# Merging two scan directions in lockstep: five groups of small products per pair, with tiles per direction

## The chip, the cores and the metric

The kernel runs on one core of one Trainium2 chip, as one launch. The metric is the time of one execution on the device in microseconds, as the median of several runs. The engines are TensorE (PE in the profile, with its weight loads as PEld), VectorE (DVE), ScalarE (ACT), GpSimd (POOL) and SyncE (SP), whose queue issues most of the transfers.

## The reference

One layer of a backbone, for 512 latent tokens and 128 context tokens (640 columns in all) of width 2048. The part that matters here:

```python
def _delta_scan(r, w, k, v, aa, bb, s0, reverse):
    def step(S, inp):
        r_t, w_t, k_t, v_t, a_t, b_t = inp
        sa = jnp.einsum('bhvk,bhk->bhv', S, a_t)
        S = S * w_t[:, :, None, :] + sa[..., None] * b_t[:, :, None, :] + v_t[..., None] * k_t[:, :, None, :]
        return S, jnp.einsum('bhvk,bhk->bhv', S, r_t)
    s_fin, ys = lax.scan(step, s0, xs, reverse=reverse)

def _rwkv7_bidir(p, s0, lp):        # 16 heads of 64, scanned forward (d = 0) and backward (d = 1)
    for d in range(2):
        ...
        y, s_fin = _delta_scan(rh, decay, kd, vh, -kk, kk * heads(a), s0[:, d], reverse=(d == 1))

def _layer(x, mod, s0, shift_fn, lp):
    h = _rmsnorm(x, lp['norm1_g']) * (1.0 + sc1) + sh1
    p = h @ lp['w_in']
    o_a, s_fin = _rwkv7_bidir(shift_fn(p[..., :C_SHIFT], lp['mu_shift']), s0, lp)
    o_b = _chunk_gmlp(jax.nn.gelu(p[..., C_SHIFT:]), lp)
    x = x + g1 * (jnp.concatenate([o_a, o_b], axis=-1) @ lp['w_out'])
    ...
    ff = (jax.nn.silu(h @ lp['w_ffn_gate']) * (h @ lp['w_ffn_up'])) @ lp['w_ffn_down']
```

## The kernel before

The program has three long parts. First the input norm and the product with `w_in`; then the scans with the product with `w_out`; then the two feed-forward products. Matrix products in full precision are made of three products of split operands (a high part and a rest), so that each step of the first part is three **wide products** of 128x320 (lines 189, 190 and 191, tile `big`). The change lies in the first part, in what the profile has from about 320 to 1110 us.

The scan is computed in chunks of 64 tokens. For each chunk and head a 64x64 triangular matrix has to be inverted. Heads are handled two at a time: a *pair* `p` is two heads on 128 partitions, and there are eight pairs, each with two directions `d` and ten chunks. For each pair three generators make the work:

- `take_k` forms the operands of the pair and the triangular matrices: products `pG` (line 650), transposes `pXT` (668), products `pW` (682). At the end of it the 16x16 diagonal blocks go out to DRAM (`dd`, line 690, on POOL's queue).
- `solve` reads them back in another layout (`mix`, line 795) and inverts the 16x16 blocks on VectorE, row by row (lines 803 and 805, tiles `mx`), for both directions at once. The result goes out as `d2` (812).
- `merge` reads `d2` into `TB` (822) and puts the blocks together, from 16 to 32 and from 32 to 64, with small products of 32x32: five groups per direction, called groups 1 to 5 here. Group 1 is `blk(A1, Tn)`, group 2 `blk(TT, M1, (0, 2))`, group 3 `blk(M1, TT)`, all at line 840 (tile `pblk`); group 4 is line 865 (`pM`), group 5 line 874 (`pT`). Each group is emptied from PSUM by ScalarE (lines 847, 868, 877) or VectorE (853, 857) before the next can use it. The result `TF` goes to the record `d_S` (879, POOL's queue), which the second part reads.

What sets the order: three `Mixer` objects hold the generators and hand out their steps between wide products. `mixM` holds `merge`. A step's yielded number is its cost, which is paid from a budget that grows at every second wide step; `yield -1.0` puts the next step off to a place that no other step shares (the last wide step of a half of a window, so that groups are at least 12 wide products apart in the code), and `yield HOLD` waits for 68 wide steps. `take_k` may run `mixM` on by itself where `GB` buffers would run out (`mixM.until`). Behind this a list scheduler orders the instructions of each engine by its own estimates, so that the order on an engine is not quite that of the code. PSUM tiles of tag `pt` have two buffers; the groups share them with the transposes `pvt`, `pw`, `ptm` and the products `psp`. `M1` and `M2` share one buffer of tag `M1`, and `TF` has one.

Of the kernel before, what the change touches and what calls it, by code (L numbers as in the profile page):

```python
# [10 lines left out]
F32 = mybir.dt.float32  # L11
F32R = mybir.dt.float32r
BF16 = mybir.dt.bfloat16
AF = mybir.ActivationFunctionType
# [5 lines left out]
P = 128  # L20
# [5 lines left out]
CH = 64  # L26
NCH = T // CH
# [17 lines left out]
SDIV = 9.0  # L45
HOLD = 68
WAIT = 20
SUBST = 4.6
MODR = 1.36
NREC = 8  # L50
# [34 lines left out]
F_R, F_G, F_X, F_Z, F_T, REC = 0, 128, 256, 384, 512, 576  # L85
# [3 lines left out]
def flow_step(ctx: ExitStack, tc, x_prompt, x_sample, state_rwkv, c, c_ctx, w_mod, b_mod,  # L89
# [4 lines left out]
    V, S, G, TE = nc.vector, nc.scalar, nc.gpsimd, nc.tensor  # L94
# [22 lines left out]
    for h in range(2):  # L117
        s = slice(CH * h, CH * h + CH)
# [34 lines left out]
    d_S = dp.tile([NPAIR, P, 2, NCH, REC], F32, name="d_S")  # L153
# [51 lines left out]
    with ExitStack() as ph:  # L205
# [92 lines left out]
        for t in range(NT):  # L298
# [7 lines left out]
            for q in range(4):  # L306
                pt = ps0.tile([P, 4, P], F32, tag="pt", name="ptx")
# [470 lines left out]
    mlo = bk.tile([P, 1], F32, name="mlo", bufs=1)  # L778
# [3 lines left out]
    A1_ = bp.tile([P, 2, NCH, 32], F32, name="A1_")  # L782
    TB = bp.tile([P, 2, NCH, 2, 32], F32, name="TB")
# [33 lines left out]
    def merge(p, d2):  # L817

        GB = pairs[p].GB
        for gq in range(8):  # L820
            b = 16 * (gq % 2)
            BQ.dma_start(TB[16 * gq:16 * gq + 16, :, :, :, b:b + 16].rearrange("p d c w b -> p (d c w) b"),
                         d2[gq].rearrange("d c w a b -> a (d c w) b"))
        for h in range(2):
            base = 64 * (1 - h)
            for d in range(2):
                S.copy(A1_[base:base + 16, d, :, 16:32], GB[d][base:base + 16, :, 16:32])
                S.copy(A1_[base + 32:base + 48, d, :, 16:32], GB[d][base + 32:base + 48, :, 48:64])
        yield HOLD
        for d in range(2):  # L830
            GBd = GB[d]
            TF = bp.tile([P, NCH, CH], F32, tag="TF", name="TF")
            Tn, TT, A1 = TB[:, d, :, 0, :], TB[:, d, :, 1, :], A1_[:, d]

            def blk(lhs, rhs, rows=range(4)):
                ps = pt_.tile([P, NCH, 32], F32, tag="pt", name="pblk")
                for cc in range(NCH):
                    for a_ in rows:
                        s = slice(32 * a_, 32 * a_ + 32)
                        TE.matmul(ps[s, cc, :], lhs[s, cc, :], rhs[s, cc, :], start=True, stop=True,  # L840
                                  tile_position=(32 * a_, 32 * a_))
# [5 lines left out]
            S.copy(M1, ps)  # L847
            yield 1.6
            yield -1.0

            ps = blk(TT, M1, (0, 2))
            for h in range(2):
                V.tensor_add(Tn[lo32(h)], ps[lo32(h)], Tn[lo32(h)])
            yield 1.6
            yield -1.0
            ps = blk(M1, TT)
            V.tensor_add(TF[:, :, 32:64], ps, TT)
            S.activation(TF[:, :, 0:32], TF[:, :, 32:64], AF.Copy, scale=mlo[:, 0:1])
            yield 1.7
            M2 = bp.tile([P, NCH, 32], F32, tag="M1", name="M2")  # L860
            yield -1.0
            ps = pt_.tile([P, NCH, 32], F32, tag="pt", name="pM2")
            for cc in range(NCH):
                for h in range(2):
                    TE.matmul(ps[hi32(h), cc, :], GBd[lo32(h), cc, 32:64], Tn[lo32(h), cc, :],
                              start=True, stop=True, tile_position=(64 * (1 - h), 64 * (1 - h) + 32))
            for h in range(2):
                S.copy(M2[hi32(h), :, :], ps[hi32(h), :, :])
            yield 1.2
            yield -1.0  # L870
            ps = pt_.tile([P, NCH, 32], F32, tag="pt", name="pT2")
            for cc in range(NCH):
                for h in range(2):
                    TE.matmul(ps[lo32(h), cc, :], M2[hi32(h), cc, :], TF[hi32(h), cc, 32:64],
                              start=True, stop=True, tile_position=(64 * (1 - h) + 32, 64 * (1 - h)))
            for h in range(2):
                S.copy(TF[lo32(h), :, 32:64], ps[lo32(h), :, :])
            yield 1.2
# [91 lines left out]
    pt_ = pbx.enter_context(tc.tile_pool(name="pt_", bufs=2, space=PSUM))  # L970
# [452 lines left out]
    with ExitStack() as ph:  # L1423
# [695 lines left out]
```

## Time and profile before

| | us |
|---|---|
| median of 3 runs | 3245.55 (3244.21 to 3252.82) |
| the profiled execution | 3255.98 |
| its span in the profile | 3254.2 |

The profiled execution is 10.43 us longer than the median. "Busy" is the time in which an engine had an instruction running; matmul ends are modelled. A row of the timeline gives the start in the span, the length, the engine, the line and the operation, with the idle time of the engine ahead of it and what ended that in brackets. A matmul of plain 32-bit floats is recorded twice, so that a group of 20 small products has x40 and one of 40 has x80; wide products are recorded once. PEclk is the granted TensorE clock as a share of full speed.

### The profile page before, as it was taken

Reading aid. Unit: us, or ns where it says so; the run is one execution under the profiler, and the core shown is the slowest. Engines: PE = TensorE matmul, PEld = TensorE weight load, DVE = VectorE, ACT = ScalarE, POOL = GpSimd, SP = SyncE. Lnnn points to the kernel's source line nnn. Section 1 sums busy time; section 2 is a strip of 40 time slices with the busy share of each in tenths; the row PEclk is TensorE's granted clock in tenths of the full one; section 3 lists DMA queues with packets and bytes.
Section 4 is the critical chain, followed back from the end, with each engine's and each line's share of the span. In section 5 each row is a group of like instructions: output and inputs, shape, how many; then the busy total and the mean of one; then the engine's idle time right before and its main releaser. Section 6 shows DMA issues by size and latency. Waiting matters only on the chain.

```text
span 3254.2 us, 72319 instructions
## 1 busy us (share of the span) xinstructions
PE 3113.8 (96%) x28216; PEld 2872.8 (88%) x28216; DVE 2365.7 (73%) x4115; ACT 1459.9 (45%) x3197; POOL 1218.3 (37%) x1065
## 2 busy tenths in 40 slices
PE   6999999999999999999999999999999999999997
PEld 3687778777777888899899999999999999999997
DVE  4548766676676677766878778777777787887788
ACT  3344444454344444345644444444444445443365
POOL 2001121211112113422356655665665645454542
PEclk9999999999999999999999999999999999999999
DMA  9666676777678588654444344344344364553453
GB/s 371 222 197 197 192 217 181 197 205 193 184 194 227 159 275 269 200 173 151 129 130 122 106 129 127 103 128 127 108 124 121 117 189 150 162 155 105 150 165 120
DMA packets 740438, 550.88 MB, mean 169 GB/s; under 512 B 141056, under 2 KB 673504, under 8 KB 731264
## 3 DMA queue, kind: packets, MB, share of 16 engines
q1 hardware_dynamic: 727136, 532.47, 54.2%
q0 software_dynamic: 10624, 13.23, 1.8%
q8 instruction: 222, 3.64, 0.5%
q14 instruction: 120, 0.98, 0.1%
q10 hardware_dynamic: 2336, 0.57, 0.1%
HBM read 437.79 MB, written 110.95 MB: 169 GB/s over the span
## 4 chain that ended last, share of the span: by engine, by line
PE 72%; DVE 10%; DMA 7%; issue 6%; POOL 3%; ACT 2%; SPq 0%; DVEq 0%; POOLq 0%; ACTq 0%
PE P L1637 15%; PE P L1635 15%; PE P L1636 15%; PE big L189 5%; PE big L191 4%; PE big L190 4%; PE pm L900 2%; DMA wt<-in_w_mod_dram 1%; DVE lo L1417 1%; PE pG L650 1%; PE big L1475 1%; PE big L1476 1%; PE big L1477 1%; PE big L1032 1%; DVE mx L803 1%
## 5 line engine op out<-in xcount | busy, mean ns | idle before, releaser
L1637 PE MATMUL P<-xo,lo 128*128 128x320 f32 x2352 | 728.0, 310 | 2.6 <-DVE lo L1417 2.5
L1635 PE MATMUL P<-xo,hi 128*128 128x320 f32 x2352 | 727.4, 309 | 0.7 <-ACT hi L1416 0.7
L1636 PE MATMUL P<-xo,hi 128*128 128x320 f32 x2352 | 727.2, 309 | 0.0
L1417 DVE TENSOR_TENSOR lo<-raw,hi 128x512 fp32r<-128x512 f32 x526 | 499.9, 954 | 178.0 <-ACT hi L1416 172.8
L1416 ACT CAST hi<-raw 128x512 fp32r<-128x512 f32 x526 | 327.0, 622 | 486.0 <-PE P L1636 384.6
L189 PE MATMUL big<-h_hi,hi 128*128 128x320 f32 x1376 | 450.9, 328 | 8.2 <-ACT hi L167 4.8
L1637 PEld LDWEIGHTS P<-xo,lo 128*128 128x128 f32 x2352 | 441.9, 188 | 4.0 <-DVE lo L1417 4.0
L1635 PEld LDWEIGHTS P<-xo,hi 128*128 128x128 f32 x2352 | 441.9, 188 | 1.0 <-ACT hi L1416 1.0
L1636 PEld LDWEIGHTS P<-xo,hi 128*128 128x128 f32 x2352 | 441.9, 188 | 0.0
L191 PE MATMUL big<-h_hi,lo 128*128 128x320 f32 x1376 | 434.2, 316 | 1.1 <-DVE lo L168 0.9
L190 PE MATMUL big<-h_lo,hi 128*128 128x320 f32 x1376 | 433.6, 315 | 0.6 <-DVE h_lo L351 0.6
L1545 POOL TENSOR_TENSOR raw<-raw 128x512 f32<-128x512 f32 x252 | 409.0, 1633 | 16.4 <-DVE lo L1417 4.9
L1637 PE MATMUL P<-xd,lo 128*128 128x320 f32 x1232 | 385.2, 313 | 18.7 <-DVE lo L1417 18.4
L1635 PE MATMUL P<-xd,hi 128*128 128x320 f32 x1232 | 383.1, 311 | 1.5 <-ACT hi L1416 0.6
L1636 PE MATMUL P<-xd,hi 128*128 128x320 f32 x1232 | 382.1, 310 | 0.0
L168 DVE TENSOR_TENSOR lo<-raw,hi 128x512 fp32r<-128x512 f32 x268 | 184.0, 689 | 204.0 <-ACT hi L167 193.6
L189 PEld LDWEIGHTS big<-h_hi,hi 128*128 128x128 f32 x1376 | 262.5, 191 | 76.2 <-issue 50.6
L1416 ACT CAST hi<-rawd 128x512 fp32r<-128x512 f32 (+1 forms) x288 | 168.8, 587 | 243.5 <-PE P L1636 206.4
L191 PEld LDWEIGHTS big<-h_hi,lo 128*128 128x128 f32 x1376 | 262.6, 191 | 10.8 <-issue 3.5
L190 PEld LDWEIGHTS big<-h_lo,hi 128*128 128x128 f32 x1376 | 263.3, 191 | 6.4 <-issue 1.7
L167 ACT CAST hi<-raw 128x512 fp32r<-128x512 f32 x268 | 165.1, 618 | 223.9 <-PE big L190 112.2
L1637 PEld LDWEIGHTS P<-xd,lo 128*128 128x128 f32 x1232 | 232.5, 189 | 25.6 <-DVE lo L1417 25.4
(403 smaller groups left out, 6109.2 us busy)
## 6 DMA issues: line engine op xcount, KB each, us to landing
wt<-in_w_mod_dram SPq DMA_DIRECT2D x96, 1024.0 KB
raw<-in_w_ffn_gate_dram SPq DMA_DIRECT2D x182, 256.0 KB
raw<-in_w_ffn_up_dram SPq DMA_DIRECT2D x182, 256.0 KB
rec<-d_S SPq DMA_DIRECT2D x80, 576.0 KB
raw<-in_w_in_dram SPq DMA_DIRECT2D x172, 256.0 KB
rawd<-in_w_ffn_down_dram SPq DMA_DIRECT2D x128, 256.0 KB
raw<-in_w_out_dram SPq DMA_DIRECT2D x96, 256.0 KB
xd<-d_os SPq DMA_DIRECT2D x66, 320.0 KB
```

The source lines that it names most:

```text
L167: S.copy(hi, raw)
L168: V.tensor_sub(lo, raw, hi.bitcast(F32))
L189: TE.matmul(halves[hf], hi[:, k, :], h_hi[:, kb, s], start=(kb == 0), stop=False)
L190: TE.matmul(halves[hf], hi[:, k, :], h_lo[:, kb, s], start=False, stop=False)
L191: TE.matmul(halves[hf], lo[:, k, :], h_hi[:, kb, s], start=False, stop=(kb == KB - 1))
L900: TE.matmul(pm[32 * j:32 * j + 2, :], cT[:, 2 * kb:2 * kb + 2], quad[:, j, :], start=(kb == 0), stop=(kb == KB - 1), tile_position=(0, 32 ...
L1416: S.copy(hi[:, 0:nk], raw[:, 0:nk])
L1417: V.tensor_sub(lo[:, 0:nk], raw[:, 0:nk], hi[:, 0:nk].bitcast(F32))
L1545: G.tensor_tensor(out=o[:, 0:nk], in0=p[:, 0:nk], in1=q[:, 0:nk], op=ALU.subtract)
L1635: TE.matmul(ps, hi[:, k, :], xk[:, 0, :], start=f, stop=False)
L1636: TE.matmul(ps, hi[:, k, :], xk[:, 1, :], start=False, stop=False)
L1637: TE.matmul(ps, lo[:, k, :], xk[:, 0, :], start=False, stop=l)
```

## The change

The loop over directions goes from outside the five groups to inside each of them. Before, a pair went through groups 1 to 5 for direction 0 and then for direction 1, ten groups with ten `yield -1.0`. Now each group makes the products of both directions, one after the other, into two PSUM buffers, then empties both; there are five groups with five `yield -1.0`, and each yields twice the former cost. `TF` and `M1` become two tiles each (tags `TF0`, `TF1`, `M10`, `M11`; 3840 more bytes in each partition). Both transfers to `d_S` and both entries of `merged` come at the end. The number and the shape of all instructions stay the same. A constant `NW` is added that nothing uses.

```diff
-        for d in range(2):
-            GBd = GB[d]
-            TF = bp.tile([P, NCH, CH], F32, tag="TF", name="TF")
-            Tn, TT, A1 = TB[:, d, :, 0, :], TB[:, d, :, 1, :], A1_[:, d]
-
-            def blk(lhs, rhs, rows=range(4)):
-                ps = pt_.tile([P, NCH, 32], F32, tag="pt", name="pblk")
+        TF = [bp.tile([P, NCH, CH], F32, tag=f"TF{d}", name="TF") for d in range(2)]
+        Tn, TT, A1 = ([t(d) for d in range(2)] for t in (
+            lambda d: TB[:, d, :, 0, :], lambda d: TB[:, d, :, 1, :], lambda d: A1_[:, d]))
+
+        def blk(lhs, rhs, rows=range(4)):
+            ps = [pt_.tile([P, NCH, 32], F32, tag="pt", name="pblk") for d in range(2)]
+            for d in range(2):
                 for cc in range(NCH):
                     for a_ in rows:
                         s = slice(32 * a_, 32 * a_ + 32)
-                        TE.matmul(ps[s, cc, :], lhs[s, cc, :], rhs[s, cc, :], start=True, stop=True,
+                        TE.matmul(ps[d][s, cc, :], lhs[d][s, cc, :], rhs[d][s, cc, :], start=True, stop=True,
                                   tile_position=(32 * a_, 32 * a_))
-                return ps
-
-            M1 = bp.tile([P, NCH, 32], F32, tag="M1", name="M1")
-            yield -1.0
-            ps = blk(A1, Tn)
-            S.copy(M1, ps)
-            yield 1.6
-            yield -1.0
-
-            ps = blk(TT, M1, (0, 2))
+            return ps
+
+        def pair_of(name):
+            return [bp.tile([P, NCH, 32], F32, tag=f"M1{d}", name=name) for d in range(2)]
+
+        M1 = pair_of("M1")
+        yield -1.0
+        ps = blk(A1, Tn)
+        for d in range(2):
+            S.copy(M1[d], ps[d])
+        yield 3.2
+        yield -1.0
+        ps = blk(TT, M1, (0, 2))
+        for d in range(2):
             for h in range(2):
-                V.tensor_add(Tn[lo32(h)], ps[lo32(h)], Tn[lo32(h)])
-            yield 1.6
+                V.tensor_add(Tn[d][lo32(h)], ps[d][lo32(h)], Tn[d][lo32(h)])
+        yield 3.2
...
-            yield 1.2
-            BQ.dma_start(d_S[p, :, d, :, F_T:F_T + CH], TF)
+        yield 2.4
+        for d in range(2):
+            BQ.dma_start(d_S[p, :, d, :, F_T:F_T + CH], TF[d])
             merged.append(p)
```

Groups 3, 4 and 5 are changed in the same way.

The scheduler's order changes beyond the groups. The first place is VectorE at the inversion of the seventh pair. In the rows `zk` and `nkk` belong to `take_k`, `mx<-mx,mix` is the first multiplication of `solve`, which needs the transfer `mix`, and `lo` is a weight's split. Before:

```order
L470 SCALAR_TENSOR_TENSOR zk<-praw,prm,zk 128x1 x2
L470 SCALAR_TENSOR_TENSOR zk<-praw,prm,zk 128x448
L168 TENSOR_TENSOR lo<-raw,hi 128x512
L803 TENSOR_TENSOR mx_1122<-mx_1121,mix 80x2
L470 SCALAR_TENSOR_TENSOR zk<-praw,prm,zk 128x448
L805 TENSOR_REDUCE mx_1121<-mx_1122 80x2
L564 TENSOR_SCALAR nkk<-zk,prm 128x640
```

The same place on VectorE now (lines up to 829 are one higher):

```order
L471 SCALAR_TENSOR_TENSOR zk<-praw,prm,zk 128x448
L563 TENSOR_TENSOR wr<-wl,wh 128x512
L471 SCALAR_TENSOR_TENSOR zk<-praw,prm,zk 128x448
L169 TENSOR_TENSOR lo<-raw,hi 128x512
L565 TENSOR_SCALAR nkk<-zk,prm 128x640
L804 TENSOR_TENSOR mx_1122<-mx_1121,mix 80x2
L806 TENSOR_REDUCE mx_1121<-mx_1122 80x2
```

The last part of `zk` and `nkk` now stand ahead of the first `mx` instruction; before, they stood behind it.

The second place is TensorE at groups 2 and 3 of the seventh pair (`pblk<-M,TB` is group 2, `pblk<-TB,M` group 3). Before, for the first direction:

```order
L840 MATMUL pblk<-M_11900,TB 32x32 x5
L668 MATMUL pXT<-ident,X 128x64 x16
L840 MATMUL pblk<-M_11900,TB 32x32 x15
L668 MATMUL pXT<-ident,X 128x64
L840 MATMUL pblk<-TB,M_11900 32x32 x13
L668 MATMUL pXT<-ident,X 128x64 x3
L840 MATMUL pblk<-TB,M_11900 32x32 x27
```

The same place on TensorE now, with both directions (`M_11901` and `M_11902`):

```order
L841 MATMUL pblk<-M_11901,TB 32x32 x20
L841 MATMUL pblk<-M_11902,TB 32x32 x20
L190 MATMUL big<-h_hi,hi 128x320
L191 MATMUL big<-h_lo,hi 128x320
L192 MATMUL big<-h_hi,lo 128x320
L841 MATMUL pblk<-TB,M_11901 32x32 x40
L190 MATMUL big<-h_hi,hi 128x320
L191 MATMUL big<-h_lo,hi 128x320
L683 MATMUL pW_11776<-Z,GA 64x64 x10
```

The transposes no longer cut group 2, the second direction stands right behind the first, and three wide products part group 2 from group 3. In the whole order, runs of small products that hold a merge group fall from 80 to 57, all runs of small products up to the last group from 287 to 275, and the changes between a merge group and other small products inside such a run from 77 to 53. From the second part on the order of TensorE is the same but for the first few rows.

More of the change, by code (lines that the diff above doesn't have):

```diff
@@ L47 @@
 WAIT = 20
+NW = 8
 SUBST = 4.6
@@ L866, in merge @@
                               start=True, stop=True, tile_position=(64 * (1 - h), 64 * (1 - h) + 32))
+        for d in range(2):
             for h in range(2):
-                S.copy(M2[hi32(h), :, :], ps[hi32(h), :, :])
-            yield 1.2
-            yield -1.0
-            ps = pt_.tile([P, NCH, 32], F32, tag="pt", name="pT2")
+                S.copy(M2[d][hi32(h), :, :], ps[d][hi32(h), :, :])
+        yield 2.4
+        yield -1.0
+        ps = [pt_.tile([P, NCH, 32], F32, tag="pt", name="pT2") for d in range(2)]
@@ L872, in merge @@
+        for d in range(2):
             for cc in range(NCH):
                 for h in range(2):
-                    TE.matmul(ps[lo32(h), cc, :], M2[hi32(h), cc, :], TF[hi32(h), cc, 32:64],
+                    TE.matmul(ps[d][lo32(h), cc, :], M2[d][hi32(h), cc, :], TF[d][hi32(h), cc, 32:64],
                               start=True, stop=True, tile_position=(64 * (1 - h) + 32, 64 * (1 - h)))
+        for d in range(2):
             for h in range(2):
-                S.copy(TF[lo32(h), :, 32:64], ps[lo32(h), :, :])
@@ L878, in merge @@
-            yield 1.2
-            BQ.dma_start(d_S[p, :, d, :, F_T:F_T + CH], TF)
+                S.copy(TF[d][lo32(h), :, 32:64], ps[d][lo32(h), :, :])
+        yield 2.4
+        for d in range(2):
+            BQ.dma_start(d_S[p, :, d, :, F_T:F_T + CH], TF[d])
             merged.append(p)
```

19 lines of the change are left out of this document (10 added, 9 removed).

## The prediction

> **What bounds the kernel now.** I read the page's busy times first, then the stretches, then TensorE's waits in the stretch of the merges.
>
> ```profile
> PE 3113.8 (96%) x28216; PEld 2872.8 (88%) x28216; DVE 2365.7 (73%) x4115; ACT 1459.9 (45%) x3197; POOL 1218.3 (37%) x1065
> 320.00:1115.00 795.00, 751.80 (x9526) 629.34 (x9525) 544.99 (x1045) 359.90 (x785) 143.09 (x230) 0.97 0.70 193
> 1115.00:3254.00 2139.00, 2081.02 (x16762) 2024.68 (x16760) 1640.77 (x2708) 974.97 (x2184) 1038.20 (x769) 0.99 0.49 149
> ```
>
> TensorE is busy for 3113.8 of 3254.2 us. In the stretch with the merges it is busy for 751.80 of 795.00 us, so it idles for 43.2 us, and its clock is granted at 0.97. Behind the stretch it is busy for 2081.02 of 2139 us in an order that hardly changes, so what the stretch gains or loses goes to the end nearly whole. The change adds and removes no instruction: its effect can only come from three places, the entering and leaving of small products, TensorE's 43.2 us of idle time, and the clock. The waits behind the idle time (us in total, times, longest):
>
> ```profile
> PE pW L682 <- ACT XT L674: 7.2, 3, 4.5
> PE ptm L175 <- issue: 4.1, 2, 3.0
> PE pm L900 <- DMA wt<-in_w_mod_dram: 3.6, 3, 2.7
> PE pblk L840 <- DVE TB L853: 2.8, 2, 1.6
> PE pblk L840 <- issue: 1.8, 2, 1.2
> PE psp L768 <- ACT TF L877: 1.8, 1, 1.8
> PE pM L865 <- DVE TB L853: 1.0, 1, 1.0
> PE pblk L840 <- ACT M L847: 0.5, 1, 0.5
> ```
>
> The merge groups themselves (pblk, pM) wait for 2.8 + 1.8 + 1.0 + 0.5 = 6.1 us in all: most of their emptying is already hidden behind wide products. So lockstep has little latency to win; I look for its gain elsewhere.
>
> **Term 1: entering and leaving.** Two wide products, group 4, two wide products:
>
> ```profile
> 1104.38 0.31 PE L190 MATMUL big<-h_lo,hi 128*128 128x320 f32 x1
> 1104.53 0.31 PE L191 MATMUL big<-h_hi,lo 128*128 128x320 f32 x1
> 1104.77 0.82 PE L865 MATMUL pM<-TB,GB 32*32 32x32 f32 x40
> 1105.52 0.42 PE L189 MATMUL big<-h_hi,hi 128*128 128x320 f32 x1
> 1105.77 0.31 PE L190 MATMUL big<-h_lo,hi 128*128 128x320 f32 x1
> ```
>
> Wide products start 0.15 us apart. From 1104.53 to 1105.77 two such steps would take 0.30; they took 1.24, so the group costs 0.94. Its 40 records run from 1104.77 to 1105.52, which is 0.75 us or 18.8 ns each; the other 0.19 us is entering and leaving. A cut inside small products costs less:
>
> ```profile
> 376.62 0.31 PE L865 MATMUL pM<-TB,GB 32*32 32x32 f32 x6
> 376.86 0.80 PE L668 MATMUL pXT<-ident,X 64*128 64x64 f32 x16
> ```
>
> Six records at 18.8 ns are 0.11 us; the next kind starts after 0.24, so 0.13 us go to the cut. The built order (counted in the section on the change) has 12 runs of small products fewer and 24 cuts fewer. That is 12 x 0.19 + 24 x 0.13 = 2.3 + 3.1 = **-5.4 us**. The bounds: 0, if the cuts hide behind weight loads, and 40 x 0.19 = -7.6, if each of the 40 joined groups saves a whole entry. I take the count, because the scheduler puts other small products where the removed groups were.
>
> **Term 2: the longest wait.** The 4.5 us of `pW` come from VectorE:
>
> ```profile
> 932.27 0.16 DVE L803 TENSOR_TENSOR mx<-mx,mix 80x2 f32<-80x2 f32 x1 [4.62 <-DMA mix<-dd]
> 933.06 0.55 DVE L564 TENSOR_SCALAR nkk<-zk,prm 128x640 f32<-128x640 f32 x1
> 933.65 0.74 ACT L566 ACTIVATE sqk<-nkk 128x640 f32<-128x640 f32 x1 [6.72 <-DVE nkk L564]
> 934.29 0.25 ACT L674 COPY XT<-pXT 128x128 f32<-128x128 f32 x1
> 934.59 1.33 PE L682 MATMUL pW<-Z,GA 64*64 64x64 f32 x20 [4.51 <-ACT XT L674]
> ```
>
> VectorE stands for 4.62 us in front of the `mx` instruction until a transfer lands. `nkk` is queued behind that, on ScalarE `sqk` behind `nkk`, the `XT` copy behind `sqk`, and TensorE waits for the copy. In the new order (first place shown with the change) `nkk` stands ahead of the waiting instruction, and on ScalarE `sqk` and the copy keep their order. VectorE will wait there still, but with nothing of TensorE's behind it. The 4.51 us go. The clock lost with them shows in windows of 3.41 us (length, PE busy, granted clock, DMA share, GB/s):
>
> ```profile
> 471.45:474.86 3.41, 2.08 (x13) 1.00 0.41 77
> 474.86:478.27 3.41, 3.41 (x52) 0.50 0.69 156
> 491.92:495.33 3.41, 1.83 (x81) 1.00 0.08 21
> 874.22:877.63 3.41, 3.41 (x105) 1.00 0.40 87
> 877.63:881.05 3.42, 3.42 (x59) 1.00 0.79 206
> 932.25:935.66 3.41, 1.07 (x20) 0.50 0.06 14
> 935.66:939.07 3.41, 3.41 (x32) 0.50 0.44 101
> 1014.17:1017.58 3.41, 2.54 (x82) 1.00 0.97 240
> 1017.58:1020.99 3.41, 3.41 (x125) 0.50 1.02 225
> ```
>
> From 932.25 to 939.07 the clock was 0.50 and TensorE busy for 1.07 + 3.41 = 4.48 us, which at full clock is 2.24. So the term is -4.51 - 2.24 = **-6.7 us**, between that and 0, if something else in the same place is late.
>
> **Term 3: the groups' own waits.**
>
> ```profile
> 468.15 0.62 PE L840 MATMUL pblk<-TB,M 32*32 32x32 f32 x48 [0.57 <-issue]
> 494.72 0.88 PE L840 MATMUL pblk<-TB,M 32*32 32x32 f32 x80 [1.58 <-DVE TB L853]
> 615.43 0.82 PE L865 MATMUL pM<-TB,GB 32*32 32x32 f32 x40 [1.02 <-DVE TB L853]
> 706.14 0.88 PE L840 MATMUL pblk<-TB,M 32*32 32x32 f32 x80 [1.23 <-DVE TB L853]
> L847 ACT COPY M<-pblk x16: 405/423/437, 324.1 to 1095.7; 128x320 f32<-128x320 f32 x16
> L853 DVE TENSOR_TENSOR TB<-pblk,TB x32: 469/485/490, 336.9 to 1100.9; 32x320 f32<-32x320 f32 x32
> ```
>
> At 615.43 no wide product stood between group 3 and group 4; now 15 do. At 468.15 it was one, now 14. At 706.14 it was 12, now 36. Those 1.02 + 0.57 + 1.23 go. Of the 1.58 at 494.72 I count half, since 14 wide products stand there now, about as many as then. Together -3.6. Against that, each group now waits for two emptyings on one engine. That is hidden where 24 or 36 wide products (3.5 or 5.3 us) part the groups, and not at four places where four to six (0.6 to 0.9 us) part group 1 from group 2: a second `M` copy, 4 x 0.42 = +1.7. At the seventh pair only three wide products part groups 2 and 3 (second place shown with the change), and two more `TB` additions, 2 x 0.49 = +1.0, are in the open. The term is **-0.9 us**, between -3.6 and, with a second copy in the open at each of the 40 joined groups, 40 x 0.42 - 3.6 = +13.
>
> The Trainium skill, page "TensorEngine Tiling (Array Packing)", section "PSUM Bottleneck", speaks against the change here: small tiles speed up TensorE but not the emptying of PSUM, and both ScalarE and VectorE should be used for it, where the new code gives both directions' copies to one engine. This trace's 0.5 us of waits for the `M` copies do not show such a limit; by the page the term would be its upper end, +13.
>
> **Term 4: edits that cost nothing.** The two `d_S` transfers wait in POOL's queue for the later direction; behind them stand the next pair's transfers, which the 68 wide steps (204 x 0.15 = 31 us) of HOLD cover; without that cover each would cost its wait. The last `psp` waited 1.8 us for `TF` copies that stand on ScalarE among the next part's casts. They still do, so I leave it at 0, between -1.8 and +1.7 (four copies of 0.42).
>
> The sum is -5.4 - 6.7 - 0.9 = -13.0 us. I give 2 us back, since a faster TensorE meets transfers like `wt` (3.6 us of waits) earlier: **-11 us**. Against the profiled execution that is 3255.98 - 11 = 3245.0; that one lay 10.43 above the median, so 3234.5 as a median.
>
> **The rivals.**
>
> Slower, through PSUM and the clock. Each group takes both `pt` buffers, so `psp`, `pvt` and `ptm` wait until a group is emptied, and TensorE takes its work in order. The price of one such meeting is that of 494.72, 1.58 us, and, where it makes a window like 471.45 or 1014.17, a window at half clock, 3.41 x 0.5 = 1.7 more. One in each of the eight pairs is 8 x 3.3 = +26; with terms 1 and 2 (-12.1) that is +14, or 3260. It decides from 2.7 us per pair on (8 x 2.7 = 12.1 + 9.7). For it: the window at 1014.17 was 2.54 us busy, mostly with small products, and the clock halved behind it. Against it: the one at 874.22 was full of small products, and the clock stayed; so did it behind 491.92.
>
> The Trainium skill, page "TensorE: Matmul & The Clock Gate", section "What's actually happening", has the clock halve only after an idle window of about 3.4 us. The rows at 471.45 and 1014.17 disagree: TensorE was busy for 2.08 and 2.54 us there and the clock halved. By the page this rival would lose its second price and come out at 8 x 1.6 - 12.1 = +1, no change.
>
> No change, since the long wait moves. If VectorE's wait for `mix` holds up something else of TensorE's, term 2 is 0 and the sum -11 + 6.7 = -4.3, or 3241. The same comes out if the joined groups do not do what they say: the scheduler cuts them again, term 1 is 0, and the sum is -5.6, or 3240. For it: group 3 of the seventh pair still stands in pieces.
>
> Faster still. If the shifted order frees three more half-clock windows (3 x 1.7 = 5.1) and `ptm`'s 4.1, it is -20, or 3225.
>
> **How the numbers follow.** About 0.3%, 9.7 us, is what a measurement of this kernel can tell from no change. The forecast has a chance of 0.42 and the faster rival 0.08: faster 0.50. The two ways to no change have 0.27, the slower rival 0.23. The low end, 3221, is term 1 at -7.6, term 2, term 3 at -3.6, term 4 at -1.8 and one more wait like `ptm`'s 3.0 with its half-clock window (1.7) gone: -24.4 in all, against the median. The high end, 3262, holds the slower rival at its one meeting per pair and leaves out what is worse.
>
> **What would show it.** In the profile after: the `pW` wait of 4.5 us gone and no half clock near 932 to 939; pblk and pM waits under 6 us in all; a double group 4 (x80) starting the next wide product 1.50 us after its start instead of twice 0.75 with two entries; the stretch about 11 us shorter, the part behind it as long as before. I am wrong if TensorE's waits for `M`, `TB` or `TF` copies grow to 15 us or more, or if the granted clock of the stretch falls under 0.97; and wrong in term 2 if VectorE's wait for `mix` reappears in front of another chain to TensorE.

## The result, and the profile after

The changed kernel takes 3273.1 us as a median, the kernel before 3245.1 in the same comparison: 1.0076 times as long, 95% interval 1.0055 to 1.0098. The prediction of 3234.5 with a range up to 3262 was wrong in sign and in range.

The busy times of the page and the two stretches, in the order of columns shown before. The first part ends later now, so its stretch goes to 1139 (the last `praw` copy of the first part ends at 1138.6; before, at 1114.3):

```profile
PE 3117.2 (95%) x28216; PEld 2874.3 (88%) x28216; DVE 2359.9 (72%) x4115; ACT 1462.9 (45%) x3197; POOL 1219.2 (37%) x1065
320.00:1139.00 819.00, 757.39 (x9520) 632.07 (x9519) 543.89 (x1044) 361.68 (x783) 142.41 (x230) 0.96 0.69 186
1139.00:3272.00 2133.00, 2078.70 (x16764) 2022.13 (x16762) 1635.73 (x2708) 975.91 (x2185) 1039.63 (x769) 0.99 0.49 150
```

About the same 9520 products took 819 us instead of 795; TensorE idles for 61.6 us instead of 43.2. The loss arises here: the first part takes 24 us more, the rest is 6 us shorter. (The two profiled executions so differ by 18 us only, where the medians differ by 28; the one before lay 10 us above its median.) The waits of TensorE that matter below (us in total, times, longest):

```profile
PE pm L911 <- DMA wt<-in_w_mod_dram: 9.9, 6, 4.3
PE pblk L841 <- issue: 6.6, 4, 2.6
PE pG L651 <- DVE GA L661: 6.6, 7, 2.8
PE pmm L519 <- DVE zv L698: 6.3, 2, 3.9
PE pW L683 <- ACT XT L675: 5.5, 4, 3.4
PE big L191 <- issue: 4.9, 1, 4.9
PE pblk L841 <- ACT vt L733: 2.7, 1, 2.7
PE pXT L669 <- ACT vt L733: 2.3, 1, 2.3
PE ptm L176 <- issue: 2.4, 2, 1.8
PE pblk L841 <- ACT M L852: 0.9, 1, 0.9
```

The emptyings that I had feared (`M`, `TB`, `TF`) stand there with 0.9 us. What grew most is "issue", time in which TensorE waited for nothing that the profile shows: `pblk` had 1.8 us of it before and `big` none. (The `issue` of `ptm` is of another kind, before and after: each time TensorE goes on 0.10 us behind the last `ms` addition on VectorE, whose result `ptm` transposes, for example at 846.84 behind the one that ended at 846.74. That is a plain wait which the profile does not name.) Five stops in the timeline, each in a joined group or a few products behind one (the first four wide products behind group 3 of the first pair):

```profile
350.64 0.31 PE L190 MATMUL big<-h_hi,hi 128*128 128x320 f32 x1
...
355.88 0.43 PE L191 MATMUL big<-h_lo,hi 128*128 128x320 f32 x1 [4.93 <-issue]
...
481.22 0.37 PE L841 MATMUL pblk<-TB,A__1119 32*32 32x32 f32 x19
483.64 0.32 PE L841 MATMUL pblk<-TB,A__1119 32*32 32x32 f32 x15 [2.04 <-issue]
...
902.60 1.38 PE L841 MATMUL pblk<-TB,M 32*32 32x32 f32 x136
906.53 0.39 PE L841 MATMUL pblk<-TB,M 32*32 32x32 f32 x24 [2.55 <-issue]
...
1043.22 0.21 PE L669 MATMUL pXT<-ident,X 64*128 64x64 f32 x1 [2.28 <-ACT vt L733]
```

The one not shown is 1.20 us at 767.59. What they have in common shows in the transfers, where one queue carries instructions (packets, MB, share):

```profile
q8 instruction: 222, 3.64, 0.5%
```

222 packets of 16,384 bytes, 3.64 MB in all: spread over TensorE's 28,216 matmul and 28,216 weight-load records that is 64 bytes an instruction and 256 instructions in a packet (222 x 256 = 56,832, which leaves 400 for its other instructions). Kernels below with 640 products fewer or 1280 more, 2560 records fewer or 5120 more, have 212 and 242 packets: 256 records for each. The single packets, read from the trace, beside TensorE's stops:

```
packet 18:  353.49 to  354.43   TensorE goes on at  355.88   1.45 us later
packet 27:  480.44 to  482.20                       483.64   1.44
packet 54:  765.14 to  766.21                       767.59   1.38
packet 67:  904.05 to  905.03                       906.53   1.50
packet 77: 1040.59 to 1041.72                      1043.22   1.50
```

Each stop ends 1.4 to 1.5 us after a packet of instructions has landed. (At the last one the profile names the `vt` copy. It had ended at 1042.92, 0.30 us earlier, where TensorE goes on 0.05 us behind a copy that it did wait for, as at 1113.22.) A joined group 1 or 3 has 160 matmul and 160 weight-load records, 320 instructions, and went through in 1.51 us; it is larger than a packet. Wide products use two instructions in 0.147 us, so there a packet lasts 19 us.

Below, "instruction stalls" are TensorE's idle times over 0.3 us that end 1.25 to 1.6 us behind such a packet. A few are other waits that fall there by chance. Where an engine really ended a wait, TensorE goes on 0.03 to 0.15 us behind that engine's instruction; so 2.3 of the 4.5 us in the kernel before are waits for VectorE (1.58 at 494.72 and 0.77 at 343.40, both 0.15 us behind the instruction that the profile names), while none of the 13.0 us after is. "Half-clock loss" is half of TensorE's busy time in windows with a granted clock of 0.50. "Work" is what is left of the time from 316.5 to the last `praw` copy without idle time and half-clock loss. The sum for the two profiles:

| us | before | after | difference |
|---|---|---|---|
| work at full clock | 734.1 | 727.8 | -6.3 |
| instruction stalls | 4.5 | 13.0 | +8.5 |
| waits for `wt` | 3.6 | 9.9 | +6.3 |
| other idle time | 35.0 | 38.7 | +3.7 |
| half-clock loss | 20.5 | 32.6 | +12.1 |
| sum | 797.7 | 822.0 | +24.3 |

Of the 32.6 us at half clock, 11.6 follow directly on the five instruction stalls (1.33 at 355, 5.12 at 485, 1.71 at 908, 3.41 at 1045, none at 768). At the first stop the packet itself began late, at 353.49, where TensorE had stopped at 350.95; the other transfers moved some 290 GB/s meanwhile. Why it began so late is not shown.

### The profile page after: what moved, and what is told of

Read it like the earlier page. It is cut to its first block, busy times and chain, and to the rows that moved or that the text cites. A ratio compares the mean times of both kernels' runs of the same rounds, so it can differ in the third digit from the quotient of the medians.

```text
span 3272.5 us, 72299 instructions
## 1 busy us (share of the span) xinstructions
PE 3117.2 (95%) x28216; PEld 2874.3 (88%) x28216; DVE 2359.9 (72%) x4115; ACT 1462.9 (45%) x3197; POOL 1219.2 (37%) x1065
## 3 DMA queue, kind: packets, MB, share of 16 engines
q8 instruction: 222, 3.64, 0.5%
## 4 chain that ended last, share of the span: by engine, by line
PE 57%; DVE 5%; issue 3%; DMA 3%; POOL 2%; ACT 1%; SPq 0%; DVEq 0%; POOLq 0%; ACTq 0%
PE P L1648 15%; PE P L1646 15%; PE P L1647 15%; DVE lo L1428 1%; PE big L190 1%; PE big L1486 1%; PE big L1487 1%; PE big L1488 1%; PE big L191 1%; PE big L192 1%; PE big L1043 1%; DMA opd<-d_op 1%; PE big L1045 1%; PE big L1044 1%; DVE xd L1713 1%
## 5 line engine op out<-in xcount | busy, mean ns | idle before, releaser
L1648 PE MATMUL P<-xo,lo 128*128 128x320 f32 x2352 | 727.8, 310 | 2.1 <-DVE lo L1428 2.0
L1646 PE MATMUL P<-xo,hi 128*128 128x320 f32 x2352 | 727.5, 309 | 0.7 <-ACT hi L1427 0.7
L1556 POOL TENSOR_TENSOR raw<-raw 128x512 f32<-128x512 f32 x252 | 408.0, 1628 | 16.3 <-DVE lo L1428 4.9
L1648 PE MATMUL P<-xd,lo 128*128 128x320 f32 x1232 | 384.7, 312 | 16.7 <-DVE lo L1428 16.6
```

What stands on the lines that cost most here:

```text
L1556: G.tensor_tensor(out=o[:, 0:nk], in0=p[:, 0:nk], in1=q[:, 0:nk], op=ALU.subtract)
L1646: TE.matmul(ps, hi[:, k, :], xk[:, 0, :], start=f, stop=False)
L1648: TE.matmul(ps, lo[:, k, :], xk[:, 0, :], start=False, stop=l)
```

## The experiments

Theory F: instructions come too slowly for a joined group. Theory P, from the prediction's slower rival: both PSUM buffers of `pt` are taken. Theory O: neither; any shift of order moves the time of this kernel, and the changed one got a bad order. Theory M came in later: VectorE's wait for `mix`.

| | median, us | ratio to the kernel before, 95% | instruction stalls | idle | half-clock loss | work |
|---|---|---|---|---|---|---|
| before | 3245.1 | | 4.5 | 43.1 | 20.5 | 734.1 |
| after | 3273.1 | 1.0076 (1.0055 to 1.0098) | 13.0 | 61.6 | 32.6 | 727.8 |
| ten places | 3248.2 | 1.0007 (0.9987 to 1.0026) | 4.9 | 38.0 | 19.8 | 730.1 |
| halves | 3248.4 | 1.0014 (1.0000 to 1.0029) | 2.4 | 46.8 | 20.5 | 727.5 |
| mixed | 3253.1 | 1.0028 (1.0011 to 1.0044) | 6.7 | 44.9 | 27.4 | 731.8 |
| before, products twice | 3310.1 | 1.0205 (1.0170 to 1.0240) | 22.3 | 73.4 | 29.0 | 755.4 |
| after, half products | 3251.5 | 1.0027 (1.0010 to 1.0043) | 2.3 | 53.9 | 23.4 | 726.4 |
| before, half products | 3234.9 | 0.9968 (0.9954 to 0.9982) | 0.8 | 39.4 | 12.7 | 724.5 |
| after, HOLD 64 | 3266.7 | 1.0060 (1.0040 to 1.0079) | 12.8 | 67.9 | 32.9 | 726.1 |
| before, HOLD 64 | 3259.2 | 1.0036 (1.0022 to 1.0050) | 2.8 | 50.2 | 19.0 | 737.2 |
| after, WAIT 32 | 3268.0 | 1.0064 (1.0040 to 1.0089) | 10.7 | 53.6 | 29.3 | 723.3 |
| before, WAIT 32 | 3260.5 | 1.0045 (1.0031 to 1.0059) | 7.0 | 43.9 | 16.1 | 731.5 |
| halves, WAIT 32 | 3274.7 | 1.0082 (1.0055 to 1.0108) | 11.2 | 52.6 | 31.9 | 722.1 |
| ten places, WAIT 32 | 3261.4 | 1.0038 (1.0016 to 1.0059) | 3.5 | 49.1 | 21.2 | 729.7 |
| after, half, WAIT 32 | 3227.9 | 0.9955 (0.9937 to 0.9973) | 0.9 | 47.7 | 16.1 | 714.9 |
| before, half, WAIT 32 | 3261.2 | 1.0049 (1.0031 to 1.0066) | 0.0 | 47.0 | 24.3 | 723.3 |
| before, WAIT 24 | 3270.4 | 1.0076 (1.0059 to 1.0094) | 1.7 | 50.5 | 32.5 | 740.0 |
| ten places, WAIT 24 | 3273.4 | 1.0088 (1.0068 to 1.0108) | 1.8 | 57.2 | 24.2 | 732.2 |
| after, again | 3275.9 | 1.0081 (1.0055 to 1.0107) | 13.1 | 61.9 | 38.3 | 728.2 |

The last four columns are of one profiled execution each, whose time lies up to 14 us from its median.

### Taking the bursts apart: ten places, halves, mixed

Ten places: lockstep, but each direction's products at their own place. For group 1 (the others alike):

```diff
-        yield -1.0
-        ps = blk(A1, Tn)
-        for d in range(2):
-            S.copy(M1[d], ps[d])
-        yield 3.2
+        for d in range(2):
+            yield -1.0
+            ps = blk1(d, A1, Tn)     # blk for one direction, one PSUM tile
+            S.copy(M1[d], ps)
+            yield 1.6
```

> The lockstep loop stays (five groups, both directions inside each, tiles per direction), but the products of each direction get a place of their own, with the former cost: ten places per pair, one PSUM buffer at a time. Theory F (instruction fetch: a joined group 1 or 3 is 160 matmul and 160 weight-load records in 1.5 us, more than the 256 that one instruction packet of 16 KB holds at 64 bytes each, so TensorE runs out of instructions): the five stalls of the changed kernel that ended 1.4 to 1.5 us after an instruction packet landed (4.93, 2.04, 1.20, 2.55, 2.28 us; 13.0 in all) fall under 4 us in sum, the half clock behind them goes too, the time comes to 3240 to 3252 us. Theory P (both PSUM buffers taken at once): the same time, since only one is taken; the 2.7 us wait of pblk for the vt copy is gone. Theory O (it is the new order of the work around the groups that costs, not the joining): the time stays at 3262 to 3275.

Halves: groups 1 and 3 keep both PSUM tiles until both are made, but in two places:

```diff
             for d in range(2):
                 for cc in range(NCH):
                     ...
+                if d == 0:
+                    yield 0.1
+                    yield -1.0
```

> The changed kernel, with groups 1 and 3 made in two places each: the first direction's products in one, the second's in the next, and both emptied only behind the second. Both PSUM buffers are so held longer than in the changed kernel, while no place has more than 160 instructions (80 matmul records). Theory F: the instruction stalls fall under 4 us in sum (13.0 before) and the time to 3242 to 3255. Theory P: pvt, pw, ptm and psp wait for the held buffers, over 12 wide products (1.8 us) or more in 16 places; TensorE's waits of pvt, ptm, psp and pblk for copies rise by 15 us or more, and the time is 3280 or above. Theory O: 3262 to 3275.

Mixed: groups 1 and 3 as in the first of these, groups 2, 4 and 5 joined as in the change.

> The changed kernel, with groups 1 and 3 made and emptied direction by direction at places of their own, and only groups 2, 4 and 5 (160 instructions for both directions) joined: seven places per pair. Theory F: instruction stalls under 4 us, half of the saved entries kept (work at full clock about 3 us under the kernel before), time 3238 to 3250. Theory P: groups 2, 4 and 5 still take both buffers, half of the loss stays: 3255 to 3265. Theory O: 3255 to 3275.

Measured: 3248.2, 3248.4 and 3253.1. The first two give back 25 of the 28 us, the third 20 where up to 3250 was expected. Instruction stalls are 4.9, 2.4 and 6.7 us, where under 4 were expected of each; 2.0 of the 2.4 are a wait that ends 0.05 us behind VectorE's `lo`. The halves decide against theory P: both buffers are held longer than in the changed kernel, and the kernel is 25 us faster. Its trace does show the price of a held buffer:

```profile
PE pM L885 <- DVE sp L770: 2.8, 2, 1.4
```

`pM` waited until `psp`'s tile was emptied, 2.8 us in all, not the 15 or more that P asks for. The Trainium skill, page "TensorEngine Tiling (Array Packing)", section "PSUM Bottleneck", says that the emptying of PSUM may become the bottleneck with small tiles; in these runs it was the smaller cost.

That a place of its own is not always far enough shows at ten places, second pair, group 1:

```profile
461.51 0.89 PE L850 MATMUL pblk<-TB,A__1119 32*32 32x32 f32 x80
...
463.18 0.89 PE L850 MATMUL pblk<-TB,A__1119 32*32 32x32 f32 x80
466.81 0.64 PE L192 MATMUL big<-h_hi,lo 128*128 128x320 f32 x1 [2.75 <-issue]
```

The scheduler left four wide products between the directions, and the stall came back, with the same mark (1.43 us behind a packet).

### Making bursts in the kernel before

```diff
-                    for a_ in rows:
+                    for a_ in 2 * list(rows) if len(rows) == 4 else rows:
```

> The kernel before, direction by direction with one PSUM buffer at a time, but each product of groups 1 and 3 is issued twice into the same place (the second overwrites the first with the same numbers): each of the 32 groups becomes 320 instructions like a joined one, and nothing else is joined. The 1280 added products take 18.9 ns each (a joined group of 80 took 1.51 us until the next wide product), 24 us, so 3269 without any further effect. Theory F: instruction stalls as in the changed kernel, where 16 such groups had 13.0 us; 32 have about 26 us, and half-clock time behind them of some 12 to 24 us more: 3300 to 3325. Theories P and O: no such stalls beyond the 4 us or so of the kernel before, 3262 to 3280.

Measured: 3310.1. Work rose by 21.3 us for the added products, instruction stalls from 4.5 to 22.3, other waits by 12.5 and half-clock loss by 8.5 (12 to 24 were expected). The first of TensorE's waits there:

```profile
PE pblk L840 <- issue: 18.8, 13, 3.4
```

Dense groups of 320 instructions starve TensorE without any lockstep and with one PSUM buffer at a time. That is F, within 4 us of the 26 expected, though from two executions only.

### Half of the products

Groups 1 and 3 make every second chunk's product; the emptying reads each twice.

```diff
-                for cc in range(NCH):
+                for cc in range(0, NCH, 2 if len(rows) == 4 else 1):
...
-            S.copy(M1[d], ps[d])
+            S.copy(two(M1[d]), even(ps[d]))
```

> The changed kernel, with places, buffers, emptyings and costs as they are, but groups 1 and 3 make only every second chunk's product (the emptying reads each of these twice, so the output is not the reference's): 160 instructions in a joined group instead of 320. 640 products are left out, at 18.9 ns 12 us, so 3261 if nothing else changes. Theory F: the instruction stalls (13.0 us in the changed kernel) fall under 4, the half clock behind them goes, 3230 to 3246. Theories P and O: 3257 to 3265.

> The kernel before with the same products of groups 1 and 3 left out, direction by direction, as the other side of the same comparison (a group has 80 instructions). All theories: the 12 us of products go, 3230 to 3236. What counts is the difference to the changed kernel with the same left out: theory F says 0 or a little under (the joined one keeps its saved entries, 6 us), theories P and O say that the joined one stays 25 us or so slower.

Measured: 3251.5 and 3234.9. The joined kernel's stalls fell from 13.0 to 2.3 us (a single one, which ends 0.06 us behind VectorE's `lo` and so is another wait), and its time by 21.6 where the products alone are 12. But it stayed 16.7 us above the other one: F explains part of the loss, not all. Its trace has VectorE in front of `mx` for 16.3 us in five places, and TensorE's waits for `pW` and `pmm` grew. That led to theory M. The changed kernel has the same pattern (VectorE at the seventh pair, and what stood behind; then the windows of 3.41 us there, with TensorE's busy time first and the granted clock third from the end):

```profile
956.68 0.16 DVE L804 TENSOR_TENSOR mx<-mx,mix 80x2 f32<-80x2 f32 x1 [5.01 <-DMA mix<-dd]
...
961.61 0.48 DVE L698 TENSOR_TENSOR zv<-pmm,zv 128x320 f32<-128x320 f32 x1
...
962.14 0.54 PE L519 MATMUL pmm<-sqk,bones 128*128 128x320 f32 x1 [3.86 <-DVE zv L698]
```

```profile
959.28:962.69 3.41, 0.55 (x3) 0.47 (x3) 3.24 (x10) 1.21 (x1) 0.00 (x0) 1.00 0.34 69
962.69:966.10 3.41, 3.41 (x12) 2.85 (x12) 2.48 (x7) 0.00 (x0) 0.00 (x0) 0.50 0.75 220
```

### Shifting everything: HOLD 64

```diff
-HOLD = 68
+HOLD = 64
```

> The changed kernel with HOLD at 64 wide steps instead of 68, which moves every merge by 4 steps against the rest and lets the scheduler find another order. Theory F: 320 instructions still come in one piece, so 8 to 18 us of instruction stalls at other places, 3258 to 3278. Theory O (this one order is unlucky): stalls and time fall where they may, as likely 3245 as 3275.

> The kernel before with the same shift of HOLD. It tells how far a mere shift of order moves the time: theory F, which puts little on order, 3240 to 3256 with at most 6 us of instruction stalls; theory O, 3255 to 3275.

Measured: 3266.7 and 3259.2. The joined kernel has 12.8 us of instruction stalls at mostly other places, the other one 2.8: the stalls belong to the joined groups, not to one order. But the kernel before lost 14 us by a shift of 4 steps, 3 us more than F had allowed for; 8.6 us of that are TensorE waiting with `pblk` for the transfer into `TB`, which 68 steps had covered.

### Taking VectorE's wait away: WAIT 32

```diff
-WAIT = 20
+WAIT = 32
```

> The changed kernel with WAIT at 32 wide steps instead of 20: the inversion (the mx chain on VectorE) is put off by 12 steps, 12 x 0.44 = 5.3 us, so that the transfer mix has landed when VectorE comes to it. In the changed kernel VectorE stood 17.1 us in front of mx, and behind it zv, nkk and with them TensorE: pmm 3.86 at 962 and 2.41 at 406, pW 3.36 at 827, 9.6 in all, each followed by half clock. Theory M (this wait is the second part of the loss): VectorE's wait for mix falls under 4 us, TensorE's pmm and pW waits under 5, time 3255 to 3264. Theory F alone: the instruction stalls (13 us) stay, so it does not fall under 3255. Theory O: anything from 3245 to 3275.

> The kernel before with WAIT at 32, the control for the two others. Its one wait for mix that reached TensorE (pW 4.51 at 934, with 2.24 of half clock) goes: theory M 3236 to 3242. Theory O (what a shift does is chance): 3245 to 3260.

> The kernel with groups 1 and 3 in two places each and emptied behind the second, and WAIT at 32: no instruction burst over 160 and no wait for mix. VectorE stood 15.3 us in front of mx there with WAIT at 20. Theories F and M together: saved entries (6 us) without the new waits, 3236 to 3244, under the kernel before. If the time stays at 3246 to 3252, mix was no part of what the halves lost.

> Lockstep with ten places per pair and WAIT at 32. VectorE stood 9.0 us in front of mx there with WAIT at 20, and TensorE's pmm and pW waits were 6.0 us. Theories F and M: 3240 to 3246. Theory O: 3245 to 3260.

Measured: 3268.0, 3260.5, 3274.7 and 3261.4. In the joined kernel the wait for `mix` is gone, the waits of `pmm` and `pW` for VectorE and ScalarE fell from 12.1 to 2.2 us, and the first part ended 16 us earlier in the profile; but the median gained only 5, less than M said. The control lost 15 us and the halves 26, all against M: something that the shift brought cost more than the wait. Joined against control is +7.4 us here, where it was +28. With WAIT 32 the halves have 11.2 us of instruction stalls. At three of the places (2.25 us at 632.00, 2.27 at 827.32, 2.31 at 1033.57) the scheduler had put both directions' products next to one another again, 160 records with no wide product between them; at two (1.70 at 373.61 and 1.83 at 482.97) 80 records stand six and twelve wide products behind other dense products.

### Both causes away, and WAIT 24

The next two kernels have half the products and WAIT 32, the last two only WAIT 24.

> The changed kernel with every second chunk's product of groups 1 and 3 left out and WAIT at 32: neither 320 instructions in one piece nor a wait for mix. Its control is the next kernel. Theories F and M together say that nothing of the loss is left: the difference to the control is between -6 (the saved entries) and +3 us, so about 3242 to 3251 (3260 of the kernel before with WAIT 32, less the 12 us of products, less up to 6). If a third cause is at work, the difference is +6 or more.

> The control: the kernel before with the same products left out and WAIT at 32. 3260.5 (with WAIT 32) less 12 us: 3246 to 3252 by every theory.

> The kernel before with WAIT at 24 wide steps, 4 x 0.44 = 1.8 us later. Theory M: the wait of 4.6 us before mx at the seventh pair shrinks to 2.9, too little to stop TensorE's pW for long; 3238 to 3246. If the loss of 15 us at WAIT 32 comes from the merges being later, a third of it comes here: 3247 to 3252.

> Lockstep with ten places per pair and WAIT at 24. Of the 6.0 us of pmm and pW waits at WAIT 20, half or more goes: 3241 to 3248. If later merges cost, 3250 to 3256.

Measured: 3227.9, 3261.2, 3270.4 and 3273.4; none as expected. The joined kernel is 33 us *faster* than its control, far outside -6 to +3. And the kernel before, with nothing changed but a hold of 24 steps for 20, is as slow as the changed kernel, with 1.7 us of instruction stalls. Its waits:

```profile
PE pW L682 <- ACT XT L674: 11.9, 6, 2.9
PE pm L900 <- DMA wt<-in_w_mod_dram: 8.2, 4, 3.8
PE big L191 <- DVE lo L168: 6.1, 4, 2.8
```

So theory O holds too: with the whole computation done, shifts of order alone cost the kernel before 14, 15 and 25 us, each through other waits and the half clock behind them. Against such a spread M can't be told apart, and I leave it open.

### The supply of instructions by itself

A kernel that leaves out the layer: TensorE in a fixed order, at least 170 wide products and a burst of small ones, with no wait inside:

```python
def phase():
    for r in range(6):
        for n in (20, 40, 60, 80, 120, 160):
            wide(170 + 13 * r)
            burst(n)
    wide(170)
phase()        # no other transfers
...            # 1200 loads of 256 KB behind one another
phase()        # the same beside them
```

> Not the layer: a kernel of its own that leaves out the whole computation. TensorE in a fixed order: at least 170 wide products (25 us), then a burst of 20, 40, 60, 80, 120 or 160 small 32x32 products (80 to 640 instructions) with no wait in them, six times each; first with no other transfers, then with a steady stream of 256 KB loads. No semaphore holds TensorE, so every idle time in or behind a burst is the supply of instructions. Theory F: bursts of 20 and 40 (80 and 160 instructions) never stall; 80 (320) stalls in some of its six places, by where the packet's edge falls, 1 to 3 us without loads and up to 5 us with them; 120 and 160 always do. If dense instructions are supplied as fast as TensorE takes them, a burst of n products takes n x 18.9 ns at every size (80: 1.5 us, 160: 3.0 us) in both phases, and theory F falls.

Measured: 12 bursts of each size. Those of 20, 40 and 60 never stopped for over 0.2 us. Of those of 80, five did: 1.30 and 1.58 us in the first phase, 2.48 and 3.31 beside the transfers (290 GB/s), and 1.92 behind the last of them, which had landed by 2460 us; the other seven ran through. All bursts of 120 and 160 stopped, for 1.64 to 2.57 us at a time in the first phase and up to 3.81 beside the transfers. TensorE's timeline, a burst of 80 that ran through, one that stopped behind it, one that stopped inside it beside transfers:

```profile
610.31 1.55 PE L49 MATMUL small<-lhs 32*32 32x32 f32 x160
611.79 1.43 PE L43 MATMUL big<-x,w 128*128 128x320 f32 x8
...
809.57 1.55 PE L49 MATMUL small<-lhs 32*32 32x32 f32 x160
811.06 0.99 PE L43 MATMUL big<-x,w 128*128 128x320 f32 x5
813.35 1.91 PE L43 MATMUL big<-x,w 128*128 128x320 f32 x12 [1.30 <-issue]
...
2044.23 1.52 PE L49 MATMUL small<-lhs 32*32 32x32 f32 x156
2049.07 0.25 PE L49 MATMUL small<-lhs 32*32 32x32 f32 x4 [3.31 <-issue]
```

All 34 stops in the two phases end 1.20 to 1.59 us behind a packet. And if each matmul record is counted with its weight load as two instructions, the number of instructions between any two of the 34 stops is a multiple of 256: a whole number of packets. So TensorE stopped at the packets' edges, and nowhere else. This is F alone: no semaphore, no emptying, no other engine. Five of twelve bursts of 80 stopped, by where the edge falls and when its packet comes.

### The changed kernel again

No edit.

> The changed kernel without an edit. Theory F: the program's packets have fixed edges, so the stalls come back at the same products (group 3 of the first pair at 356, group 1 of the second at 484, of the fifth at 768, of the sixth at 907, the transposes at 1043), each within a microsecond of its size, 10 to 15 us in all; the time is 3266 to 3276. If they were chance, they stand elsewhere or are gone.

Measured: 3275.9, and in its profile 13.1 us of instruction stalls. All five are back at the same products, behind the same packets by number (18, 27, 54, 67 and 77): 4.58 us at 354.85, 1.32 at 481.71, 1.56 at 771.40, 2.42 at 910.05, 1.43 at 1044.84 (the first time 4.93, 2.04, 1.20, 2.55, 2.28). Two new ones stand beside them, 1.10 us in the joined group 3 of the second pair and 0.63 at 1071.94. So the places are fixed by the program, as F says; whether and how long TensorE stops there also hangs on when the packet comes.

## Why the prediction was wrong

**What bounds the kernel** was right (TensorE, and a loss in the first part goes to the end whole), but the sentence that the effect "can only come from three places" failed: the supply of instructions is a fourth. The sign of it stood among the rows that I quoted, `pblk <- issue` with 1.8 us, and I passed over it: its two waits, 0.57 us at 468.15 and 1.21 at 1083.53, end 1.37 and 1.38 us behind a packet. Of the signs of being wrong that I had named, the granted clock of the stretch came, 0.96, and the wait for `mix`; the 15 us of waits for copies did not.

**Term 1** (-5.4): work at full clock fell by 6.3, near the forecast, but that does not show the account behind it. The price of an entry was too small, since I counted all the time from a group's start to the next wide product as the products' own. A joined group 4 of the changed kernel:

```profile
506.85 0.31 PE L192 MATMUL big<-h_hi,lo 128*128 128x320 f32 x1
507.09 1.45 PE L872 MATMUL pM<-TB,GB 32*32 32x32 f32 x80
508.47 0.42 PE L190 MATMUL big<-h_hi,hi 128*128 128x320 f32 x1
508.72 0.31 PE L191 MATMUL big<-h_lo,hi 128*128 128x320 f32 x1
```

The next wide product starts 1.38 us after the group's start, not the forecast 1.50. By the same sum as in the prediction this group costs 1.57 us where two single ones cost 2 x 0.94, so a joined pair saves 0.31, not 0.19. And "work" moves as much without joined groups: it is 730.1 with ten places, and between 731.5 and 740.0 where only HOLD or WAIT of the kernel before was changed. Between a joined kernel and its counterpart it is 6 to 11 us lower in four of five pairs (HOLD 64: -11.1, WAIT 32: -8.2, half and WAIT 32: -8.4), in one 1.9 higher.

**Term 2** (-6.7) failed at "with nothing of TensorE's behind it". The wait of 4.51 us at 934 and its half clock are gone, but VectorE's wait came back with 5.01 us at 956.68, now in front of `zv`, and TensorE's `pmm` stood 3.86 us and ran at half clock behind it. That is the rival "the long wait moves". The same wait of 4.64 us at 824.14 stopped `pW` for 3.36.

**Term 3** (-0.9, up to +13) had its waits about right (`pblk` for copies 3.6 us) and left out what decided. The 1.58 us at 494.72, my price for a meeting at PSUM, was what the profile calls it: VectorE's second `TB` addition ended 0.15 us before TensorE went on, as at the waits of 615.43 and 706.14. But such meetings did not come. Joined groups cost +8.5 us of instruction stalls, and 11.6 of half clock behind them; with 8.5 + 11.6 - 6.3 = 13.8 us they alone turn the gain into a loss. (Without the two waits for VectorE that the 4.5 us hold, the 8.5 are 10.9.)

**Term 4**: the last `psp` no longer waits, within its bounds. The 2 us given back for `wt` were 6.3, with more half clock behind; what made these waits longer is not shown.

**The slower rival** had the direction and the half clock (+12.1 in the sum) and half the size of the loss (+14 of +28), but the wrong mechanism, so what it had right was luck: of the meetings at PSUM there is one of 2.74 us, at the last pair, not one in each. The high end, 3262, was one cause short.

What is shown and what is not: that joined groups of 320 instructions starve TensorE is shown by the four profiles with such groups (10.7 to 13.1 us, and 22.3 with all 32 doubled), against 0 to 7.0 in the others (the halves with WAIT 32 excepted, where the scheduler joined some groups again), and by the bursts alone. That taking them apart gives 25 us back is measured, at this one setting of HOLD and WAIT. That all of the 28 us come from them is not shown: in the profile they make 20.1 (8.5 + 11.6) before the saved entries, and the kernel's order, moved by HOLD or WAIT alone, is worth 14 to 25. No version tried that does the whole computation is faster than the kernel before.

## What to carry to other kernels

Count instructions, not only time: a dense run of small products must be shorter than what the instruction queue has at hand (here 60 products in a row were safe, 80 by luck, 120 never), and between two runs there must be enough wide products for the next packet (four and twelve were too few at two places). An idle time that the profile puts down to "issue" is worth a look at the instruction packets, and at what ended just before it: `ptm`'s was an ordinary wait. And where a schedule's constants were fitted to one order, measure what a mere shift costs (here up to 25 us) before giving a change the blame or the credit for a difference of that size.

## What the runs showed of the hardware

TensorE's instructions came in packets of 16 KB, 256 instructions; in dense small products it used one up in 1.2 us (320 in 1.48 to 1.51 us), while the packets ahead of the stops took 0.9 to 1.8 us on their way and 1.2 to 1.6 more passed until TensorE went on. The Trainium skill, page "Runtime: NRT & Kernel Launch", section "Instruction fetch mechanics", has the refill in such blocks, which the 222 packets bear out, and calls the fetch hidden, since instructions are issued more slowly than they are filled in; the bursts of 120 and 160 disagree.

How much idle time halves the clock shows best in the bursts kernel, which has windows of 3.41 us with little else in them (TensorE busy, then granted clock):

```profile
845.48:848.89 3.41, 1.66 (x67) 1.62 (x67) 0.00 (x0) 0.00 (x0) 0.00 (x0) 1.00 0.02 5
848.89:852.31 3.42, 3.42 (x15) 3.42 (x15) 0.00 (x0) 0.00 (x0) 0.00 (x0) 0.50 0.00 0
883.03:886.44 3.41, 1.86 (x84) 1.82 (x84) 0.00 (x0) 0.00 (x0) 0.00 (x0) 1.00 0.02 5
886.44:889.85 3.41, 3.41 (x25) 3.41 (x24) 0.00 (x0) 0.00 (x0) 0.00 (x0) 1.00 0.00 0
```

All 20 full-clock windows there with 1.72 us of idle time or more were followed by one at 0.50, and none with 1.54 or less: the edge lies near half of the window. So a stall of 2 us can cost 1.7 more for each window that the clock stays at half: one behind the stop at 906.53, two behind 1043.22 and three behind 483.64, though TensorE was busy all through them; why two and three is not shown. The Trainium skill, page "TensorE: Matmul & The Clock Gate", section "What's actually happening", asks for a whole idle window of about 3.4 us; half of one was enough. In the layer the edge is not as clean: the clock halved behind the windows at 471.45 and 1014.17 of the kernel before with 1.33 and 0.87 us idle, and I can't say why.

A group's entry costs more than I had worked out, as the joined group 4 above shows. In the bursts kernel, a burst of 20, 40, 60 or 80 takes 0.48, 0.82, 1.15 and 1.48 us from its start to the next wide product: 16.7 ns for a product and 0.15 us that do not depend on their number. My 0.19 comes on top: from the wide product before a burst of 20 to the second one behind it 0.97 us pass, and without two steps of 0.147 and the 0.48 that leaves 0.20. So a burst's fixed price is 0.35 us there.
